# Four scalings and the convolution taps of a two-layer decoder trunk given out later

## The chip, the cores and the metric

The kernel runs on one core of one Trainium2 chip. The metric is device microseconds of one execution, and lower is better. The kernel before took 253.13 us (median of 3 runs, 252.58 to 253.38).

## The reference, cut to what matters

Two layers, each a pre-norm mixer over 256 tokens of width 1024. One input projection feeds two groups, whose outputs are joined, projected and added to the residual:

```python
h = rms_norm(x, norm_g); z = h @ w_in
# group A, width 512: gated linear recurrence
cx  = causal_depthwise_conv(rg_x, conv_w, conv_b)        # 4 taps along the tokens
r, i = sigmoid(cx @ w_r + b_r), sigmoid(cx @ w_i + b_i)  # 8 diagonal blocks of 64
a   = exp(-8 * r * softplus(-lam)); u = sqrt(1 - a*a) * (i * cx)
y_a = scan(h_t = a_t * h_(t-1) + u_t) * silu(rg_gate)
# group B, 8 query heads on 2 kv heads of 64: three attention branches
y_b = (g0 * o_compressed + g1 * o_selected + g2 * o_window) * silu(nsa_gate)
x = x + concat(y_a, y_b) @ w_out
```

At 256 tokens the selected and the window branch both see every earlier token, so each is a causal softmax over 256 keys with keys, values and a gate of its own. Products with the large weights are computed to nearly full fp32 precision as three products of a high part and a low part.

## The kernel before, in words

**Tiling.** Each layer is a list of 33 steps, and each step has one chunk of weights (128 partitions by up to 1024 columns): 13 for q, k, v and the compression inputs (`tm1`, `cmp_prod`, `tm2`), 12 "feature" chunks (`fm`, here slots 0 to 11: four for the recurrence input x0 to x3, then gate chunks), and 8 for the output projection (`out_proj`; the first four are slots 12 to 15). A feature chunk is 24 matmuls of 256 columns. Its low part `wl` is made by VectorE (L168) from the raw chunk and the high part `wh`, which ScalarE makes (L165) in slots 0 to 3 and a DMA makes from slot 4 on. The low parts are made some steps ahead; for slots 2 to 5 they stand behind the last `qs` write (L383) of the first or second half of q and k.

**What else runs in the slots.** Smaller pieces are hung into slots by `at(n, f)`: ahead of the slot's products, or, with `mid=True`, behind the loads that the slot gives out.

- `qk_transpose(t)` for the two halves t of the tokens, ahead of slots 0 and 2: TensorE transposes k and q (L369, L378) into two banks of the pool `pp` (which has two), ScalarE casts them (`kd` L373 and L374, twice each; `qs` L382, twice), VectorE makes the low parts (`kl` L375, `qs` L383), and ScalarE copies q (`qT`, L385).
- `att_scores(i, t)`: score matmuls (L579 to L581) into banks of `s` (three), the maximum on VectorE (L584, L586), and four exponentials on ScalarE (L592). Pair (0, 0) is in slot 1, pairs (0, 1) and (1, 0) in slot 3.
- `att_coef(i, t)`: a reciprocal and a product on VectorE (L597, L598), and four scalings of the probabilities on ScalarE (L605). Before, that of (0, 0) is given out in the middle of slot 1.
- `att_turn(i, t)`: four transposes of the probabilities per 128 keys on TensorE (L618) into a bank of `pp`, and their copy (L83). That of (0, 0) is ahead of slot 2.
- `cmp_act` (slot 2) and `cmp_kv` (slot 3): hidden layer of the compression, with a tanh `hth` (L468), the product `hs` (L470) on VectorE and the matmuls L475 and L476 on it.
- `rg_x(j)` behind the products of slot j: VectorE evicts x_j to `xpad` (L646; two buffers, taken in turn), ScalarE makes the tap of the newest token (`cx`, L647), VectorE adds the three others (L649). `rg_gates(j)`, ahead of slot 2 + j, multiplies `cx` with the gate weights (L657) and takes tanh and exp on ScalarE (L660 to L664).

**What sets the order.** The engines run their queues in order. The queues are filled by a planner that goes through modelled time: on each engine it takes, among the instructions that it holds ready, the one written first. So an instruction that is written later can stand ahead of one that was not yet ready in the model, and moving a statement changes the precedence of its instructions rather than fixing their places.

Of the kernel before, what the change touches and what calls it, by code (L numbers as in the profile page):

```python
# [38 lines left out]
for _n, _w in (("g", 8), ("cw", 16), ("cb", 4), ("br", 4), ("bi", 4), ("lam", 4)):  # L39
# [13 lines left out]
SL = dict(qk=(0, 2), order=("x0", "x1", "x2", "x3", "n0", "n1", "g0", "g1", "g2", "g3", "n2", "n3"),  # L53
          cmp=(2, 3, 4), att=(1, 3, 3, 4, 6, 7, 10, 11), turn=(2, 4, 5, 6, 8, 10,
          12, 13), cs=(5, 5), cpt=6, aout=(6, 7, 12, 15), gates=(2, 3, 4, 5), tab=6, sqrt=5,
          scan=8, rout=(9, 11))
# [15 lines left out]
def hybrid_trunk_kernel(ctx: ExitStack, tc: tile.TileContext, vx, wc, wt, wv, wf, wo, w1, w2, pe,  # L72
# [14 lines left out]
    def act(shape, tag, bufs=1, dt=F32):  # L87
        return ap_.tile(shape, dt, name=tag, tag=tag, bufs=bufs)
# [16 lines left out]
    xpad = [cp.tile([P, S + 4], F32, name=f"xpad{c}") for c in range(2)]  # L105
# [75 lines left out]
    def v(l, n, j=None):  # L181
        a, b = VEC_COLS[n]
        if j is not None:
            a, b = a + j, a + j + 1
        return vec[:, l, a:b]
# [70 lines left out]
    def layer(l, prev):  # L256

        L = Layer()
# [381 lines left out]
        def rg_x(j):  # L640
            if j == 0:
                L.cx = act([P, 4, S], "cx")
                L.rr = act([P, 4, S], "rr")
                L.tl = act([P, 4, S], "tl")
            cx, xp = L.cx, xpad[j % 2]
            V.tensor_tensor(xp[:, 4:], L.o[:, :S], L.rb[:, 0], op=ALU.mult)  # L646
            A.activation(cx[:, j], xp[:, 4:], AF.Identity, scale=v(l, "cw", 12 + j), bias=v(l, "cb", j))  # L647
            for k in range(3):
                V.scalar_tensor_tensor(cx[:, j], xp[:, 1 + k:1 + k + S], v(l, "cw", 4 * k + j), cx[:, j],  # L649
                                       op0=ALU.mult, op1=ALU.add)  # L650
# [115 lines left out]
        order = [(o[0], int(o[1])) for o in SL["order"]]  # L766
        base = {"x": 0, "g": 4, "n": 8}
        post = {"x": rg_x, "g": rg_gate, "n": nsa_gate}
        plan = [([], []) for _ in range(16)]

        def at(n, f, *a, mid=False):
            plan[n][1 if mid else 0].append(F(f, *a))
# [6 lines left out]
        for q in range(8):  # L779
            i, t = divmod(q, 2)  # L780
            n = SL["att"][q]
            at(n, att_scores, i, t)
            at(n, att_coef, i, t, mid=True)
        at(SL["cs"][0], cmp_scores)
        at(SL["cpt"], cmp_pt)
        for q in range(8):
            at(SL["turn"][q], att_turn, *divmod(q, 2))
        for i in range(4):
            at(SL["aout"][i], att_out, i)
            at(SL["gates"][i], rg_gates, i)  # L790
        at(SL["tab"], next_gains, mid=True)
        at(SL["sqrt"], rg_sqrt, mid=True)
# [17 lines left out]
    for l in range(DEPTH):  # L810
        prev, st_ = layer(l, prev)
        prev0 = prev0 or prev
        steps += st_
# [140 lines left out]
```

## Time and profile before

| what | value |
| --- | --- |
| median of 3 runs | 253.13 us |
| profiled execution | 252.82 us |
| its span, first to last instruction | 251.0 us |
| TensorE busy with matmuls / with weight loads | 243.0 / 222.2 us |
| VectorE, ScalarE, GpSimd busy | 195.8, 164.5, 40.1 us |
| granted TensorE clock | 1.0 over the whole span |
| memory read | 55.78 MB |

The profiled execution is 1.8 us longer than its span. Busy times are shares of the span and say how full an engine is on the mean; what an engine waited for is in the views of waits, and the order in which its queue was filled is in the timelines. In the first layer slots 0 to 5 lie at about 38 to 74 us, in the second at about 158 to 196 us.

### The profile page before, as it was taken

To read this page: it belongs to the slowest core of one execution; us is meant where nothing else is said; L and a number is where in the kernel's file an instruction comes from. 1 tells how busy PE (TensorE), PEld (TensorE's weight loads), DVE (VectorE), ACT (ScalarE), POOL (GpSimd) and SP (SyncE) were. 2 spreads that over 40 slices of the span, in tenths; PEclk is the share of its full clock that TensorE was granted. 3 is DMA by queue.
4 is the path that set the end of the run, shared out by engine and by line. 5 is a ranking of instruction groups with operands and counts; after the bars stand their busy time and mean duration, and the time that the engine had idled before them with its cause. 6 is when DMAs were issued, how large, how long until landed. Compare 5 with 4: busy or idle time off the path is not lost.

```text
span 251.0 us, 5217 instructions
## 1 busy us (share of the span) xinstructions
PE 243.0 (97%) x1958; PEld 222.2 (88%) x1958; DVE 195.8 (78%) x386; ACT 164.5 (66%) x419; POOL 40.1 (16%) x65
## 2 busy tenths in 40 slices
PE   7999998999999999999999999998999999999994
PEld 3989997977899798999999999996889879989993
DVE  4898798879999997654995569688999998765422
ACT  5966419799999967622873553849999996670000
POOL 0034460001811011000001044100100001010000
PEclk9999999999999999999999999999999999999999
DMA  6987999856699688562569878475249858833022
GB/s 211 371 289 226 318 413 407 265 168 202 195 322 403 184 266 293 174 202 72 167 207 347 312 236 263 159 230 187 93 167 347 317 177 268 271 127 84 3 84 84
DMA packets 17593, 57.17 MB, mean 228 GB/s; under 512 B 2208, under 2 KB 3360, under 8 KB 17056
## 3 DMA queue, kind: packets, MB, share of 16 engines
q1 hardware_dynamic: 12816, 39.86, 46.4%
q0 software_dynamic: 4608, 16.78, 20.9%
q8 instruction: 15, 0.25, 0.4%
q10 hardware_dynamic: 144, 0.20, 0.2%
q14 instruction: 10, 0.08, 0.1%
HBM read 55.78 MB, written 1.05 MB: 226 GB/s over the span
## 4 chain that ended last, share of the span: by engine, by line
PE 59%; DVE 19%; ACT 12%; DMA 4%; issue 2%; POOL 1%; SPq 0%; DVEq 0%; ACTq 0%
PE fm L173 11%; PE fm L175 10%; PE fm L174 10%; DVE wl L168 6%; PE s L174 4%; PE s L175 4%; PE s L173 4%; ACT pr L592 3%; PE m L628 3%; PE pp L618 3%; DMA raw<-in_wt_dram 2%; DMA raw<-in_wf_dram 2%; DVE cx L649 2%; POOL st L179 1%; DVE sm L584 1%
## 5 line engine op out<-in xcount | busy, mean ns | idle before, releaser
L168 DVE TENSOR_TENSOR wl<-raw,wh 128x1024 fp32r<-128x1024 f32 (+4 forms) x67 | 74.4, 1117 | 7.9 <-PE pp L174 3.0
L173 PE MATMUL fm<-hh,wh 128*128 128x256 f32 x192 | 56.9, 296 | 0.2
L174 PE MATMUL fm<-hl,wh 128*128 128x256 f32 x192 | 55.0, 287 | 0.0
L175 PE MATMUL fm<-hh,wl 128*128 128x256 f32 x192 | 54.5, 284 | 0.5 <-DVE wl L168 0.5
L165 ACT CAST wh<-raw 128x768 fp32r<-128x768 f32 (+4 forms) x35 | 30.8, 883 | 28.6 <-DMA raw<-in_wc_dram 7.6
L173 PEld LDWEIGHTS fm<-hh,wh 128*128 128x128 f32 x192 | 36.7, 191 | 2.1 <-issue 1.2
L175 PEld LDWEIGHTS fm<-hh,wl 128*128 128x128 f32 x192 | 36.7, 191 | 1.2 <-DVE wl L168 0.8
L174 PEld LDWEIGHTS fm<-hl,wh 128*128 128x128 f32 x192 | 36.7, 191 | 0.5 <-issue 0.4
L592 ACT ACTIVATE pr<-s,sm 128x128 f32<-128x128 f32 (+1 forms) x64 | 26.0, 417 | 9.4 <-DVE sm L586 6.0
L173 PE MATMUL fm<-yy,wh 128*128 128x256 f32 x96 | 27.4, 285 | 0.0
L175 PE MATMUL fm<-yy,wl 128*128 128x256 f32 x96 | 26.8, 279 | 0.0
L174 PE MATMUL fm<-yy,wh 128*128 128x256 f32 x96 | 26.8, 279 | 0.0
L605 ACT ACTIVATE pr<-pr,sm 128x128 f32<-128x128 f32 (+1 forms) x64 | 23.7, 455 | 1.8 <-DVE sm L598 1.8
L173 PEld LDWEIGHTS fm<-yy,wh 128*128 128x128 f32 x96 | 18.0, 188 | 1.5 <-DVE sm L597 0.8
L156 POOL DMA_DIRECT2D wh<-in_wo_dram x16 | 8.5, 530 | 66.2 <-PE fm L175 29.1
L174 PEld LDWEIGHTS fm<-yy,wh 128*128 128x128 f32 x96 | 18.1, 188 | 0.0
L175 PEld LDWEIGHTS fm<-yy,wl 128*128 128x128 f32 x96 | 18.0, 188 | 0.0
L174 PE MATMUL s<-wl,hh 128*128 128x384 f32 x48 | 16.5, 344 | 0.3 <-DVE wl L168 0.3
L723 DVE TENSOR_TENSOR head<-head,fm 128x512 f32<-128x512 f32 x11 | 7.5, 686 | 11.5 <-PE fm L175 11.5
L156 POOL DMA_DIRECT2D wh<-in_wf_dram x16 | 9.0, 565 | 46.2 <-PE fm L175 24.4
L175 PE MATMUL s<-wh,hl 128*128 128x384 f32 x48 | 16.2, 337 | 0.0
L173 PE MATMUL s<-wh,hh 128*128 128x384 f32 x48 | 15.6, 353 | 0.3 <-ACT wh L165 0.3
(205 smaller groups left out, 615.0 us busy)
## 6 DMA issues: line engine op xcount, KB each, us to landing
raw<-in_wf_dram SPq DMA_DIRECT2D x24, 512.0 KB, 4.5
wh<-in_wf_dram POOLq DMA_DIRECT2D x16, 512.0 KB, 4.8
raw<-in_wo_dram SPq DMA_DIRECT2D x16, 512.0 KB, 5.0
wh<-in_wo_dram POOLq DMA_DIRECT2D x16, 512.0 KB, 4.5
raw<-in_wt_dram SPq DMA_DIRECT2D x15, 384.0 KB, 3.9
yy<-in_w_dram SPq DMA_DIRECT2D x4, 1024.0 KB, 7.4
raw<-in_wc_dram SPq DMA_DIRECT2D x4, 512.0 KB, 5.2
raw<-in_wv_dram SPq DMA_DIRECT2D x4, 420.0 KB, 4.9
```

The source lines that it names most:

```text
L156: G.dma_start(self.wh, self.src)
L165: A.copy(hi[:, c], self.raw[:, c])
L168: V.tensor_tensor(lo[:, c], self.raw[:, c], hi[:, c].bitcast(F32), op=ALU.subtract)
L173: T.matmul(o, lh, rh, start=start, stop=False)
L174: T.matmul(o, lh, rl, start=False, stop=False)
L175: T.matmul(o, ll, rh, start=False, stop=stop)
L592: A.activation(pr[g][:, b], ov[:, b], AF.Exp, bias=sm[:, 0, 2 * g + b:2 * g + b + 1], accum_out=sm[:, 1, 2 * g + b:2 * g + b + 1])
L605: A.activation(pr[g][:, b], pr[g][:, b], AF.Copy, scale=sc_)
L618: T.transpose(pp[:, (2 * g + b) * P:(2 * g + b + 1) * P], pr[g][:, b, c * P:(c + 1) * P], ident)
L628: T.matmul(yb[g * HD:(g + 1) * HD, :S], L.vv[:, 0, b, g * HD:(g + 1) * HD], pt[:, g, b, 0:2].rearrange("p a s -> p (a s)"), start=(b == 0) ...
L649: V.scalar_tensor_tensor(cx[:, j], xp[:, 1 + k:1 + k + S], v(l, "cw", 4 * k + j), cx[:, j], op0=ALU.mult, op1=ALU.add)
L723: V.tensor_tensor(x_sb[:, m], x_sb[:, m], os_[0].rearrange("p (a s) -> p a s", a=2), op=ALU.add)
```

## The change

The four scalings of the first pair of probabilities, with their reciprocal and product, go from the middle of slot 1 to the head of slot 2, behind the second half of q and k (and behind `cmp_act`, which is hung there before). The three VectorE taps of each x_j become a piece of their own, `rg_conv(j)`: those of x0 and x1 go to the head of slot 2, those of x2 to slot 3, those of x3 to slot 4. The eviction and the newest token's tap stay behind the products of slot j. The head of slot 2 now reads, in order: `qk_transpose(1)`, `cmp_act`, `att_coef(0, 0)`, `att_turn(0, 0)`, `rg_conv(0)`, `rg_gates(0)`, `rg_conv(1)`. The heads of slots 3 and 4 end in `rg_gates(1)`, `rg_conv(2)` and in `rg_gates(2)`, `rg_conv(3)`. Both layers are changed alike, and no instruction is added or dropped.

```diff
             V.tensor_tensor(xp[:, 4:], L.o[:, :S], L.rb[:, 0], op=ALU.mult)
             A.activation(cx[:, j], xp[:, 4:], AF.Identity, scale=v(l, "cw", 12 + j), bias=v(l, "cb", j))
+
+        def rg_conv(j):
+            cx, xp = L.cx, xpad[j % 2]
             for k in range(3):
                 V.scalar_tensor_tensor(cx[:, j], xp[:, 1 + k:1 + k + S], v(l, "cw", 4 * k + j), cx[:, j],
                                        op0=ALU.mult, op1=ALU.add)
...
             at(n, att_scores, i, t)
-            at(n, att_coef, i, t, mid=True)
+            if q == 0:
+                at(SL["qk"][1], att_coef, i, t)
+            else:
+                at(n, att_coef, i, t, mid=True)
...
         for i in range(4):
             at(SL["aout"][i], att_out, i)
+            at(max(i + 1, 2), rg_conv, i)
             at(SL["gates"][i], rg_gates, i)
```

## Rows read from the trace of the kernel before

**Rows 1.** The page: busy time of each engine, then the chain by engine.
```profile
PE 243.0 (97%) x1958; PEld 222.2 (88%) x1958; DVE 195.8 (78%) x386; ACT 164.5 (66%) x419; POOL 40.1 (16%) x65
...
PE 59%; DVE 19%; ACT 12%; DMA 4%; issue 2%; POOL 1%; SPq 0%; DVEq 0%; ACTq 0%
```

**Rows 2.** Busy time by stretch; columns: stretch, length, each engine's busy us.
```profile
42.00:64.00 22.00, 21.20 (x203) 18.38 (x202) 19.03 (x43) 19.85 (x61) 3.10 (x6) 1.00 0.72 234
163.00:184.00 21.00, 19.87 (x162) 17.05 (x152) 18.75 (x43) 17.50 (x57) 2.20 (x4) 1.00 0.55 176
64.00:120.00 56.00, 56.00 (x479) 51.01 (x478) 45.55 (x80) 40.12 (x108) 9.61 (x17) 1.00 0.71 233
```

**Rows 3.** TensorE's waits, 42 to 64 us, then 163 to 184 (total, times, longest).
```profile
PE pp L618 <- DVE kl L375: 0.5, 1, 0.5
PE s L579 <- ACT pr L592: 0.3, 1, 0.3
...
PE m L475 <- DVE hs L470: 0.8, 1, 0.8
PE pp L618 <- DVE kl L375: 0.3, 1, 0.3
```

**Rows 4.** Timeline of TensorE, first layer; columns: start, duration, instruction, [idle before].
```profile
51.68 0.28 PE L174 MATMUL fm<-hl,wh 128*128 128x256 f32 x1
51.80 0.28 PE L175 MATMUL fm<-hh,wl 128*128 128x256 f32 x1
52.59 0.63 PE L618 MATMUL pp<-cst,pr 128*128 128x128 f32 x4 [0.50 <-DVE kl L375]
52.97 0.36 PE L173 MATMUL fm<-hh,wh 128*128 128x256 f32 x1
```

**Rows 5.** Timeline of VectorE, first layer.
```profile
44.54 1.22 DVE L168 TENSOR_TENSOR wl<-raw,wh 128x1024 fp32r<-128x1024 f32 x1
45.68 0.48 DVE L649 SCALAR_TENSOR_TENSOR cx<-xpad,head,cx 128x256 f32<-128x256 f32 x1
46.19 0.69 DVE L586 TENSOR_REDUCE sm<-s 128x4 f32<-128x512 f32 x1
...
50.98 1.00 DVE L649 SCALAR_TENSOR_TENSOR cx<-xpad,head,cx 128x256 f32<-128x256 f32 x2 [1.39 <-ACT cx L647]
52.01 0.43 DVE L375 TENSOR_TENSOR kl<-pp,kd 64x256 fp32r<-64x256 f32 x1
```

**Rows 6.** Timeline of ScalarE, first layer.
```profile
48.77 0.36 ACT L374 CAST kd<-pp 64x256 fp32r<-64x256 f32 x1
49.16 1.28 ACT L605 ACTIVATE pr<-pr,sm 128x128 f32<-128x128 f32 x4
50.34 0.60 ACT L647 ACTIVATE cx<-xpad,head 128x256 f32<-128x256 f32 x1
...
51.35 0.37 ACT L374 CAST kd<-pp 64x256 fp32r<-64x256 f32 x1
51.75 0.58 ACT L382 CAST qs<-pp 64x512 fp32r<-64x512 f32 x1
52.23 0.30 ACT L468 ACTIVATE hth<-m 128x160 f32<-128x160 f32 x1
```

**Rows 7.** Timeline of TensorE, second layer.
```profile
171.78 0.28 PE L175 MATMUL fm<-hh,wl 128*128 128x256 f32 x1
172.87 0.30 PE L475 MATMUL m<-w2s,hs 128*32 128x64 f32 x2 [0.82 <-DVE hs L470]
173.42 0.63 PE L618 MATMUL pp<-cst,pr 128*128 128x128 f32 x4 [0.25 <-DVE kl L375]
```

**Rows 8.** The chain that ended last, second layer: start, us, what.
```profile
167.32 1.51 ACT pr L592 x8
...
169.47 1.28 ACT pr L605 x4
```

**Rows 9.** Timeline of VectorE, second layer.
```profile
172.50 0.32 DVE L470 SCALAR_TENSOR_TENSOR hs<-hth,m 128x160 f32<-128x160 f32 x1
```

## The prediction

> **What bounds the kernel now.** I read four views, in this order. The busy table [rows 1] shows TensorE full (243.0 of 251.0 us) and the chain by engine puts 59% of the span on it; VectorE and ScalarE follow with 19% and 12%. So the end is the length of TensorE's queue plus the stalls in it, and only a stall taken out, or a new one, moves the end. The table by stretches says where there are stalls: from 64 to 120 us TensorE is busy all 56.00 us, while from 42 to 64 it idles 22.00 - 21.20 = 0.80 and from 163 to 184 it idles 21.00 - 19.87 = 1.13 [rows 2]. These two stretches are slots 1 to 4 of each layer, where the moved instructions are. There ScalarE is the next fullest (19.85 of 22.00 and 17.50 of 21.00), VectorE close to it. TensorE's waits name four: the transposes L618 of the first pair (both layers), L475 on `hs` (second layer), a score matmul on a bank that the exponentials still hold (first layer) [rows 3].
>
> What the reader is to see in the timelines is the queue order behind the waits. In the first layer ScalarE runs one half of `kd` (to 49.1), then the four scalings (49.16, 1.28 us), then x1's newest tap (50.34), and only then the other half of `kd` (to 51.7) [rows 6]. VectorE, meanwhile, stands 1.39 us at the taps of x1, which need that newest tap; `kl`, which frees the bank for L618, is queued behind two of them and starts at 52.01 [rows 5]. L618 then starts at 52.59, the matmul ahead of it at 51.80; matmuls of that kind follow each other at 0.12 us (51.68, 51.80), so the stall is 0.79 - 0.12 = 0.67 us [rows 4]. In the second layer the scalings again stand ahead (169.47 to 170.75) [rows 8], the tanh and `hs` come behind them (172.50) [rows 9], and TensorE stands 172.87 - 171.78 - 0.12 = 0.97 us for `hs` and 0.25 us more for L618 [rows 7].
>
> [...] TensorE's busy row gives 0.80 + 1.13 = 1.93 us of idle time in the two stretches. [...] The sum below stands on gaps between starts.
>
> **The change, part by part.** The profiled execution took 252.82 us (span 251.0, 1.8 around it); the median of the runs is 253.13, 0.31 above it. The sum is made against 252.82 and 0.31 is added at the end. Nothing is added or removed: 2 x 4 scalings and 2 x 12 taps change their precedence. No DMA is in a moved piece; SP and GpSimd keep their order and see only weight buffers come free at other times.
>
> *Scalings behind the second half of q and k.* ScalarE's steps are, from starts, 0.40 for a `kd` cast (51.35 to 51.75) and 0.48 for a `qs` cast (51.75 to 52.23); the newest tap is 0.60, the tanh 0.30, [rows 6]; `qT` I put at 0.48 like `qs`, an estimate. First layer: the second `kd` cast starts at 48.77, when the transposes have come, and two casts follow at once instead of after 1.28 us of scalings and a tap: three casts end at 48.77 + 1.20 = 49.97, `kl` (0.43) at 50.4 instead of 52.44. The newest tap, two `qs`, `qT` and the tanh end at 49.97 + 0.60 + 0.96 + 0.48 + 0.30 = 52.3, the scalings at 52.3 + 1.28 = 53.6. So the bank is free 2 us sooner, but the probabilities are ready 1.0 us later than L618 started before. What is late next is thus L618's own data. The cover: in the model L618 is then not ready when slot 2's products are, so it falls behind them; six of them (L173 at 52.97 and five more, 0.72 us at 0.12 [rows 4]) and the scores of pair (0, 1) are there to be run, whose `qs` is ready at 51.5 + 0.69 (VectorE's part) = 52.2, before the products end at 51.92 + 0.72 = 52.6. With the cover the 0.67 us go; without it L618 stalls TensorE 1.0 us longer. Bounds +0.67 and -1.0; I take 0.67, because the queue of before shows the planner running products ahead of transposes that were not ready.
>
> Second layer: the exponentials end at 167.32 + 1.51 = 168.83 [rows 8]. If they end 0.5 sooner (next part), four casts, tap, two `qs`, `qT` and tanh (1.60 + 0.60 + 0.96 + 0.48 + 0.30 = 3.94) end at 172.25, and `hs` (0.32) at 172.6: 0.2 us before its old end of 172.82. That is the low bound, with the tanh last. If the planner takes the tanh ahead of `qT`, or the scores of pair (0, 1) ahead of L475, the 0.97 + 0.25 = 1.22 us go whole. I take the middle, 0.7.
>
> *Taps a step later.* They cost VectorE the same 0.48 each. One goes from in front of the maximum of the first scores (45.68, maximum at 46.19 [rows 5]; the second layer repeats it), which can start a tap's 0.51 us earlier: bounds 0, if the planner fills the place with this or another tap, and 1.14, if a `wl` in front goes too. I take 0.5; it feeds ScalarE, which waits for that maximum, and is inside the figures above. The 1.39 us that VectorE stands at x1's taps go, since `kl`, `qs` and `hs` now precede them. Later taps make the gate products L657 later. I cost that at nothing: slots 3 to 5 have matmuls that do not need them, and the recurrence is used only in slots 9 and 11. If that cover is gone, the taps of x3 are late by the low part put in front of them, 1.14 us (44.54 to 45.68 [rows 5]) per layer. x2's eviction has to wait for x0's taps (same `xpad`); VectorE has from 46.9 us to the end of slot 2's products at 52.6 for three.
>
> *The score matmul that waits for its bank* (0.3 us [rows 3]) I leave as it is: it can go (0.3), because scores of (0, 1) start earlier, or grow by what TensorE comes earlier (0.67).
>
> Sum: 0.67 + 0.7 = 1.4 us; 252.82 - 1.4 = 251.4, and with 0.31, **251.7 us**.
>
> **The rivals.**
>
> *A: given back behind it, no change.* ScalarE is nearly full in the two stretches [rows 2], so TensorE, arriving 1.4 us earlier, may meet exponentials, copies and the compressed branch that come no earlier, and stand there instead. What ScalarE can gain is only its idle time there, 2.15 and 3.50 us. For it: the wait for the exponentials is already there. Against it: from 64 us on TensorE runs 56 us without idling, so it has other matmuls to take. It gives 0 to -0.5: 252.9 us.
>
> *B: slower, L618 stands at its old place in the queue.* Mechanism: the model thinks the scalings are done when L618's turn comes, and on the chip they end at 53.6, 1.0 us after L618's old start (the working is above). TensorE then idles from 51.92 to 53.6, in the first layer 1.0 us more than before; in the second the scalings end at 172.25 + 1.28 = 173.5 against 173.42, 0.1 more. It decides when fewer than 1.7 us of other matmuls (53.6 - 51.9) stand between slot 2's product at 51.80 and L618. Price 1.1: 252.82 + 1.1 + 0.31 = 254.2 us. For it: before, too, L618 stood in the queue ahead of slot 2's last six products and held them up [rows 4]. [...]
>
> *C: the order on the chip hardly changes,* because the planner takes what is ready and the casts are not, when the scalings are. Against it: the second `kd` pair comes from the same bank as the first, which ran ahead of the scalings [rows 6]. 253.1 us.
>
> **How the numbers follow.** Forecast 0.55, A 0.20, B 0.17, C 0.08. The likeliest alone reaches from 250.6 (all four waits gone, 0.67 + 1.22 + 0.3 = 2.2, and a little from the earlier maximum) to 252.5 (0.67 + 0.2, less 0.3 of a grown wait). For 8 in 10 the range takes in A, C and the near part of B: 250.5 to 253.9. About 0.3% (0.76 us) is what a measurement of this kernel can tell from no change. Faster 0.56, within 0.30, slower 0.14 (B, less its mildest part).
>
> **What would show it.** Right: on ScalarE four `kd` casts without a scaling between them, in both layers; `kl` two us sooner; no idle VectorE at x1's taps; L618 behind slot 2's last product, and no wait over 0.3 us for `hs` or L618. Wrong: L618 waiting for L605 (B); waits for exponentials or for the compressed branch that were not there (A); gate products waiting for `cx` on TensorE, which would make the tap part cost what I put at nothing. If the waits go and the time stays, the sum over stalls was the wrong measure.

## The result and the profile after

The changed kernel takes 254.45 us (median of 20 runs, 252.85 to 255.31); the kernel before, run beside it, 252.75 us (20 runs, 251.77 to 253.51). The ratio is 1.0058, 95% interval [1.0041, 1.0076]: by it the change is 1.5 us slower, where 1.4 us less was forecast. The time lies 0.55 us above the range; of the cases, rival B (254.2) is the nearest. Of the runs further down, one execution each of e7 (295.63 us, at a granted clock of 0.755), of e12 (394.82 us, at 0.561) and of the kernel before (828.99 us, beside e9 to e12) is far slower than the others of its kernel; the ratios, means and counts leave it out, the medians are over all runs.

The profiled execution took 253.98 us (span 252.2). Its page first: the busy row, the granted clock in 40 slices, and the chain by engine. They answer to [rows 1].

```profile
PE 244.1 (97%) x1958; PEld 223.7 (89%) x1958; DVE 196.2 (78%) x386; ACT 164.6 (65%) x419; POOL 40.0 (16%) x65
...
PEclk9999999999999999999999999998999999999999
...
PE 79%; ACT 9%; DVE 8%; issue 2%; DMA 1%; ACTq 0%
```

TensorE is still what sets the end, with 79% of the chain. Its busy time has grown by 1.1 us although no instruction was added, and one slice of the clock row, that from 170.2 to 176.5 us, is not full. The view by stretches, which answers to [rows 2], has both:

```profile
42.00:64.00 22.00, 20.83 (x172) 17.85 (x162) 20.08 (x47) 20.17 (x64) 4.50 (x9) 1.00 0.68 231
163.00:184.00 21.00, 19.29 (x130) 16.45 (x126) 17.22 (x41) 16.52 (x54) 2.20 (x4) 0.92 0.49 151
64.00:120.00 56.00, 55.77 (x476) 50.63 (x475) 44.46 (x75) 38.87 (x103) 8.27 (x13) 1.00 0.70 228
```

TensorE idles 1.17 us in the first layer's stretch (0.80 before) and 1.71 in the second's (1.13 before), and in the second's the mean granted clock is 0.92. TensorE's waits in the first layer (two rows), then in the second, which answer to [rows 3]:

```profile
PE pp L618 <- ACT pr L605: 0.8, 1, 0.8
PE m L497 <- DVE sm L598: 0.3, 1, 0.3
...
PE pp L618 <- DVE kl L375: 1.7, 1, 1.7
```

The wait of L475 for `hs` and that for the score bank are gone. The transposes L618 still wait, and longer: in the first layer now for the scalings, in the second for `kl`. (Lines from L649 on stand 3 lower than before: the taps are L652, the gate products L660.) TensorE's timeline in the first layer, beside [rows 4]:

```profile
49.68 0.28 PE L174 MATMUL fm<-hl,wh 128*128 128x256 f32 x1
50.73 0.33 PE L618 MATMUL pp<-cst,pr 128*128 128x128 f32 x1 [0.78 <-ACT pr L605]
50.82 0.36 PE L175 MATMUL fm<-hh,wl 128*128 128x256 f32 x1
...
51.26 0.28 PE L175 MATMUL fm<-hh,wl 128*128 128x256 f32 x1
51.64 0.33 PE L618 MATMUL pp<-cst,pr 128*128 128x128 f32 x1
```

The matmul at 49.68 is the 11th of slot 2's 24 products; before, L618 stood behind the 18th. The queue gives the four transposes out one by one between products, and TensorE stands 50.73 - 49.68 - 0.12 = 0.93 us at the first and 0.26 at the second. In the second layer, beside [rows 7], L618 stands behind the 18th product; before, it stood behind all 24 and L475:

```profile
170.50 0.28 PE L175 MATMUL fm<-hh,wl 128*128 128x256 f32 x1
172.49 0.78 PE L618 MATMUL pp<-cst,pr 128*128 128x128 f32 x4 [1.71 <-DVE kl L375]
...
174.54 0.77 PE L579 MATMUL s<-kd,qs 128*128 128x512 f32 x1
175.11 0.63 PE L580 MATMUL s<-kl,qs 128*128 128x512 f32 x1
175.54 0.44 PE L581 MATMUL s<-maskb,identb 128*128 128x256 bf16 x1
...
177.94 0.38 PE L660 MATMUL fm<-cx,rws 128*128 128x256 f32 x1
```

The stall is 172.49 - 170.50 - 0.12 = 1.87 us. What follows it is slow as well: from L579 to the gate product the scores take 177.94 - 174.54 = 3.40 us. The same instructions of the kernel before:

```profile
174.03 0.48 PE L579 MATMUL s<-kd,qs 128*128 128x512 f32 x1
174.34 0.40 PE L580 MATMUL s<-kl,qs 128*128 128x512 f32 x1
174.58 0.28 PE L581 MATMUL s<-maskb,identb 128*128 128x256 bf16 x1
...
176.03 0.60 PE L657 MATMUL fm<-cx,rws 128*128 128x256 f32 x2
```

There they take 2.00 us. The granted clock, by stretches of the changed kernel (the column behind the five engines), says why:

```profile
163.00:174.20 11.20, 9.49 (x77) 8.74 (x73) 9.38 (x18) 7.93 (x26) 0.53 (x1) 1.00 0.58 184
174.20:177.60 3.40, 3.40 (x13) 2.26 (x13) 2.18 (x5) 3.02 (x11) 1.10 (x2) 0.50 0.53 145
177.60:184.00 6.40, 6.40 (x44) 5.45 (x43) 5.66 (x20) 5.58 (x21) 0.57 (x1) 1.00 0.30 95
```

For 3.4 us, from 1.7 us after the stall's end on, TensorE's granted clock is 0.50 in place of 1.00, and the scores take 3.40 - 2.00 = 1.40 us longer. It is not in every run. Twelve of the 20 runs have a mean granted clock of 0.992 or 0.993 and a mean time of 254.68 us; the other eight have 0.998 or more and 253.53. The mean of the kernel before is 252.76. So of the mean loss of 1.46 us, 0.77 is there without the low clock, and 0.6 x 1.15 = 0.69 comes with it.

Why `kl` is late is in ScalarE's and VectorE's timelines of the second layer:

```profile
167.28 0.21 ACT L592 ACTIVATION_READ_ACCUMULATOR pr<-s,sm 128x1 f32 x1
168.26 0.40 ACT L605 ACTIVATE pr<-pr,sm 128x128 f32<-128x128 f32 x1 [0.78 <-DVE xpad L646]
168.57 0.35 ACT L373 CAST kd<-pp 64x256 fp32r<-64x256 f32 x1
168.82 0.60 ACT L647 ACTIVATE cx<-xpad,head 128x256 f32<-128x256 f32 x1
169.45 0.36 ACT L374 CAST kd<-pp 64x256 fp32r<-64x256 f32 x1
169.84 0.58 ACT L382 CAST qs<-pp 64x512 fp32r<-64x512 f32 x1
...
170.52 0.39 ACT L605 ACTIVATE pr<-pr,sm 128x128 f32<-128x128 f32 x1
170.94 0.37 ACT L373 CAST kd<-pp 64x256 fp32r<-64x256 f32 x1
171.32 0.37 ACT L374 CAST kd<-pp 64x256 fp32r<-64x256 f32 x1
```

```profile
167.81 0.42 DVE L646 TENSOR_TENSOR xpad<-fm,rb 128x256 f32<-128x256 f32 x1
169.46 0.48 DVE L652 SCALAR_TENSOR_TENSOR cx<-xpad,head,cx 128x256 f32<-128x256 f32 x1 [1.23 <-ACT cx L647]
169.86 0.41 DVE L375 TENSOR_TENSOR kl<-pp,kd 64x256 fp32r<-64x256 f32 x1
...
171.92 0.43 DVE L375 TENSOR_TENSOR kl<-pp,kd 64x256 fp32r<-64x256 f32 x1
```

The four `kd` casts (L373, L374, once for each 64 rows) don't follow each other. The pair of the second 64 rows comes 1.1 us behind the first pair (169.81 to 170.94; in the first layer it is the same, 48.19 to 49.31), after `kl` of the first 64 rows (ends at 170.27). In the program the second L373 waits for VectorE's first `kl`: e5 below, which writes the casts ahead of the differences, closes the gap (there the second L373 starts at 169.53, 0.38 us behind the L374 at 169.15). (Both read one bank of `pp`, and they share the tile `kd`; no run shows which of the two makes the cast wait.) On the chip ScalarE does not stand in the gap, since a `qs` cast, the tanh and a single scaling are queued in it. It stands at the start: the exponentials end at 167.49, but a scaling is queued ahead of the first cast and waits 0.78 us, by the trace for VectorE's eviction of x1 (L646), so the first cast starts at 168.57, 1.08 us behind the exponentials. The 1.23 us that VectorE stands at x1's tap hold `kl` up very little: it starts at 169.86, 0.05 us behind the end of the cast that it needs. From the start of the second half's L369 to the end of the last `kl` it takes 4.10 us in the first layer (before 4.46) and 5.67 in the second (before 6.05): 0.4 us less in each.

### The profile page after: what moved, and what is told of

Same layout as the page of the kernel before. It is cut to its first block, busy times and chain, and to the rows that moved or that the text cites. A ratio compares the mean times of both kernels' runs of the same rounds, so it can differ in the third digit from the quotient of the medians.

```text
span 252.2 us, 5214 instructions
## 1 busy us (share of the span) xinstructions
PE 244.1 (97%) x1958; PEld 223.7 (89%) x1958; DVE 196.2 (78%) x386; ACT 164.6 (65%) x419; POOL 40.0 (16%) x65
## 4 chain that ended last, share of the span: by engine, by line
PE 79%; ACT 9%; DVE 8%; issue 2%; DMA 1%; ACTq 0%
PE fm L173 13%; PE fm L174 12%; PE fm L175 12%; PE s L173 5%; PE s L174 5%; PE s L175 5%; PE pp L618 4%; PE m L628 3%; DVE wl L168 2%; PE s L579 2%; PE fm L660 2%; PE s L580 2%; PE pp L175 2%; PE pp L173 2%; PE pp L174 2%
## 5 line engine op out<-in xcount | busy, mean ns | idle before, releaser
L605 ACT ACTIVATE pr<-pr,sm 128x128 f32<-128x128 f32 (+1 forms) x64 | 24.3, 448 | 4.0 <-DVE sm L598 3.3
L618 PE MATMUL pp<-cst,pr 128*128 128x128 f32 x96 | 15.4, 276 | 2.6 <-DVE kl L375 1.7
```

The source lines that it names most:

```text
L605: A.activation(pr[g][:, b], pr[g][:, b], AF.Copy, scale=sc_)
L618: T.transpose(pp[:, (2 * g + b) * P:(2 * g + b + 1) * P], pr[g][:, b, c * P:(c + 1) * P], ident)
```

## The experiments

All were timed beside the kernel before, on three chips (252.40 us beside e1 to e4, 252.50 beside e9 to e12, 252.57 beside the others). In the table, the first-layer stretch goes from the start of the second half's L369 to the first product of the second layer, and the second-layer stretch from the same L369 to the last attention output (from there to the last matmul it is 27.24 us in every kernel). The stall is the longest one in slots 2 to 4 of the second layer, between starts and less the usual step. "Low" counts runs with a mean granted clock under 0.995; where a profiled execution has 0.997 to 0.999 (e4, e5, e6, e9), its clock is 1.00 from 42 to 64 us and from 160 to 190. Stretches and stalls are of one execution, times of all. The two stretches do not add up to the span, because what lies ahead of them varies: the L369 with which the first one begins starts at 47.98 us in the kernel before, at 46.41 in the changed kernel and at 47.34 in the same kernel once more (e13). Whether a part of that belongs to the change is not shown.

| kernel | median us, ratio | layer 1 | layer 2 | stall | low |
| --- | --- | --- | --- | --- | --- |
| before | | 79.38 | 52.69 | 0.97 | 0 of 84 |
| changed | 254.45, 1.0058 [1.0041, 1.0076] | 80.40 | 54.40 | 1.87 | 12 of 20 |
| changed again (e13) | 254.90, 1.0083 [1.0061, 1.0105] | 80.57 | 54.32 | 1.86 | 4 of 6 |
| scalings only (e2) | 252.87, 1.0018 [1.0000, 1.0036] | 79.92 | 52.79 | 1.35 | 0 of 12 |
| taps only (e3) | 252.80, 1.0011 [0.9994, 1.0028] | 79.45 | 52.70 | 1.58 | 0 of 12 |
| L618 in slot 3 (e1) | 252.13, 0.9981 [0.9964, 0.9999] | 79.33 | 52.57 | 0.57 | 0 of 12 |
| so in layer 1 only (e12) | 252.81, 1.0006 [0.9984, 1.0027] | 79.15 | 52.57 | 1.60 | 0 of 10 |
| so in layer 2 only (e11) | 254.04, 1.0059 [1.0044, 1.0074] | 80.12 | 52.85 | 0.58 | 0 of 5 |
| before, L618 in slot 3 (e4) | 253.60, 1.0045 [1.0025, 1.0065] | 80.43 | 52.74 | 0.95 | 0 of 12 |
| stall filled (e9) | 256.62, 1.0166 [1.0130, 1.0201] | 80.60 | 55.42 | 0.46 | 1 of 6 |
| its control (e10) | 253.78, 1.0066 [1.0043, 1.0089] | 81.57 | 52.83 | 1.88 | 4 of 10 |
| casts freed (e5) | 253.46, 1.0033 [1.0017, 1.0048] | 80.11 | 53.10 | 1.36 | 0 of 12 |
| before, casts freed (e6) | 253.30, 1.0038 [1.0016, 1.0059] | 80.46 | 52.84 | 1.29 | 0 of 12 |
| L618 in slot 3, casts freed (e7) | 251.77, 0.9956 [0.9935, 0.9978] | 79.27 | 52.12 | 0.94 | 0 of 11 |

**Is it L618's place in the queue?** e1: the changed kernel, with the transposes of (0, 0) a slot later in both layers.

```diff
-          cmp=(2, 3, 4), att=(1, 3, 3, 4, 6, 7, 10, 11), turn=(2, 4, 5, 6, 8, 10,
+          cmp=(2, 3, 4), att=(1, 3, 3, 4, 6, 7, 10, 11), turn=(3, 4, 5, 6, 8, 10,
```

> The changed kernel with the transposes of the first pair (L618) hung ahead of slot 3 instead of slot 2, so that in TensorE's queue they stand behind slot 2's 24 products and the scores of slot 3, in both layers. Theory P (place): the loss is L618 standing too early in TensorE's queue (1.87 us in the second layer, some 1.2 in the first) and the fall of the granted clock behind the second stall. Then both stalls and the fall go: 251.2 to 252.3 us, granted clock 1.0 in every run, slot 3's first product in the second layer some 2.5 us earlier than in the changed kernel. Rival S (ScalarE): the interleaved scalings and casts make ScalarE's chain late and TensorE waits for it wherever L618 stands: 253.5 to 254.5, with waits for kl, hs or exponentials of 1 us or more in slot 3. Rival T (taps): late taps hold the gate products: 253.5 to 254.5, with waits for cx.

252.13 us: by the ratios to the kernel before, 0.9981 and 1.0058, it is 0.8% (1.9 us) under the changed kernel, and a little under the kernel before. TensorE's timeline of e1, first layer:

```profile
52.15 0.28 PE L175 MATMUL fm<-hh,wl 128*128 128x256 f32 x1
52.35 0.30 PE L475 MATMUL m<-w2s,hs 128*32 128x64 f32 x2
...
52.83 0.48 PE L579 MATMUL s<-kd,qs 128*128 128x512 f32 x1
...
54.83 0.60 PE L618 MATMUL pp<-cst,pr 128*128 128x128 f32 x4
```

L618 comes behind the products and the scores, and nothing stands between. The order of ScalarE's and VectorE's casts, scalings and taps in these slots is that of the changed kernel; what differs is where L618 is queued, and its copy, and in the second layer a wait of ScalarE that is 0.27 us shorter (as in e12 below). So, with the casts and scalings in this order, the place is the cause of the stalls: L618 ahead of matmuls that could run, as rival B had it. (The products alone are not cover enough: in e3's second layer and in e6's first, L618 stands behind all 24 of them but ahead of the scores, and TensorE stands 1.58 and 1.00 us.) What is left is 0.57 us at L497 in the second layer and 0.44 at the gate products, for `cx`, in the first.

e4: the same edit on the kernel before.

> The kernel before with L618 of the first pair hung ahead of slot 3. In the first layer it then stands behind all 24 products, in the second behind L475 and a group of scores. Theory P: the old L618 stalls (0.67 and 0.25 us) go and the wait for hs in the second layer (0.97) stays: 251.8 to 252.5. Rivals S and T: no change from before, 252.5 to 253.0.

A miss: 253.60, slower than before. TensorE now stands at the first score, for VectorE's `qs`, which there has taps in front of it:

```profile
53.41 0.49 PE L618 MATMUL pp<-cst,pr 128*128 128x128 f32 x3
54.36 0.50 PE L579 MATMUL s<-kd,qs 128*128 128x512 f32 x1 [0.46 <-DVE qs L383]
```

In the second layer the 0.95 for `hs` stays. So the change and the later transposes pay only together: each alone loses (ratios 1.0058 and 1.0045), both gain a little (0.9981, with an interval that ends just under 1).

**Which part loses?** e2 leaves the taps as they were, e3 the scalings.

```diff
-            at(max(i + 1, 2), rg_conv, i)
```

(e2, with the taps back in `rg_x`)

> Only the scalings are moved, the taps stand as before. L618 then stands behind 14 of slot 2's 24 products in the first layer and 19 in the second (the changed kernel: 11 and 18; before: 18 and all 24). Theory P: most of the loss stays, 253.3 to 254.5, a stall of 1 to 2 us at L618 in the second layer, and a fall of the clock behind it in part of the runs. Rival T (taps): no loss, 252.3 to 253.0. Rival S: like P in time, but with the wait at exponentials, not at L618.

```diff
-            if q == 0:
-                at(SL["qk"][1], att_coef, i, t)
-            else:
-                at(n, att_coef, i, t, mid=True)
+            at(n, att_coef, i, t, mid=True)
```

(e3)

> Only the taps are moved, the scalings stand as before. L618 then stands behind 15 of 24 products in the first layer and behind all 24 in the second. Theory P: about the kernel before, 252.2 to 253.2, since the second layer's stall is at most the old one, and no fall of the clock. Rival T: the loss is here, 253.7 to 254.6. Rival S: as before, 252.5 to 253.0, as the scalings are not touched.

Both lose little, 0.47 and 0.40 us, and neither is set apart from no change with any margin. For e2 that is a miss: I had put most of the loss on the scalings. e3's time came as expected, its stall not. With each part alone the second layer's longest stall is longer (1.35 and 1.58 us, both at L618 for `kl`; before 0.97, at L475 for `hs`), and in neither is a run at the low clock. Their sum, 0.87, is near the 0.77 that the changed kernel loses in its runs at 0.998 or more, but each is uncertain by some 0.45 us. The other 0.69 appears only with both.

**Which layer?** e12 and e11 move the transposes in one layer.

```diff
-            at(SL["turn"][q], att_turn, *divmod(q, 2))
+            at(3 if q == 0 and not l else SL["turn"][q], att_turn, *divmod(q, 2))
```

(e12; e11 has `and l`)

> The changed kernel with L618 of the first pair ahead of slot 3 in the first layer alone. Theory P: the second layer's stall and the fall of the clock stay, 253.2 to 254.4, at most 1.2 us under the changed kernel. Rival (the first layer carries it): 252.2 to 252.8.

> The changed kernel with L618 of the first pair ahead of slot 3 in the second layer alone. Theory P (the place of L618 is the loss, and it is the second layer's stall with the clock that counts): 252.2 to 253.0, clock 1.0. Rival: the first layer's stall of 0.94 and 0.27 us carries as much: 253.3 or more.

Both missed, since I had put most of the loss on the second layer. With the first layer mended (e12) the time is that of the kernel before, and the first-layer stretch is 1.25 us shorter than the changed kernel's; the second layer's stall stays, at 1.60 us, and costs nothing that its stretch shows (52.57, before 52.69), as no run has the low clock. With the second layer mended (e11) the loss stays. So the first layer carries a loss in every run, and the low clock, where a profile shows it, lies behind the second layer's stall. That stall is 0.27 us shorter in e12 although the second layer is written as in the changed kernel: in e12 (and in e1) the scaling ahead of the first cast doesn't wait for the eviction of x1,

```profile
167.92 0.40 ACT L605 ACTIVATE pr<-pr,sm 128x128 f32<-128x128 f32 x1 [0.50 <-DVE sm L598]
```

and the last `kl` ends 5.40 us behind the L369, not 5.67. So e12 changed the second layer's stall as well, and can't say which of its two changes keeps the clock up. e11's 254.04 is 1.5 us above before, where its stretches add up to 0.9; the rest I can't place, and five runs are few.

**Is it the low clock behind the stall?** e9 fills the second layer's stall with sixteen products of 256 columns of zeros, which change no result; e10 is the same without them.

```diff
+                if k == 5 and L.fill:
+                    L.fill = False
+                    for _ in range(16):
+                        T.matmul(L.o[:, S:], wz[:, :P], wz, start=False, stop=False)
+                    att_turn(0, 0)
...
```

(Not shown is the part that arms this in the second layer alone and takes the old place out.)

> The changed kernel, in the second layer L618 tied behind 18 of slot 2's 24 products (where it stands in the changed kernel anyway), and 16 matmuls of 256 columns by zeros put in front of it, into an unused half of the products' bank. They fill the 1.87 us that TensorE stood there (16 by about 0.11 = 1.8 us) and add nothing else. Theory G (the granted clock falls because TensorE stood idle): the stall is filled, the clock stays at 1.0 in every run, and the time is that of the changed kernel's runs without a fall, 252.9 to 253.7. Rival H (the clock falls for another reason, such as what the chip does in that stretch): it falls in most runs as before, 254.0 to 255.3.

> The control of the filled kernel: the same tie of L618 behind 18 products in the second layer, without the matmuls by zeros. Theories G and H both: a stall of 1.6 to 2.0 us at L618, a fall of the clock in half or more of the runs, 253.8 to 255 in the median.

e10 is much like the changed kernel, with 253.78 us and four low runs of ten both just under what I had expected. Its first-layer stretch is 1.2 us longer than the changed kernel's, mostly since the gate products wait 1.07 us for `cx` there, so it is a control for the second layer alone. Its profiled execution has the stall, 1.88 us, but the stretch that had a clock of 0.50 there has 1.00 here (four others of its ten runs have a mean of 0.993):

```profile
174.20:177.60 3.40, 3.40 (x25) 2.42 (x23) 3.27 (x6) 3.38 (x9) 0.53 (x1) 1.00 0.18 24
```

And its second-layer stretch is 52.83, only 0.14 above before. So the wait at L618 by itself takes the place of the two waits that it removed; it is the clock, with the 1.40 us above, that makes it dear. e9 fills the gap and has no fall of the clock behind it in its profile (1.00 from 160 to 190 us), but the time is a miss, 256.62. The fill changed the order behind it: VectorE makes three `wl` in one go ahead of the next maxima.

```profile
175.48 3.49 DVE L168 TENSOR_TENSOR wl<-raw,wh 128x1024 fp32r<-128x1024 f32 x3
```

So e9 says something of the clock and nothing of the time.

**Is it the casts' interlock?** e5 issues both halves' casts ahead of VectorE's differences, for `kd` and for `qs` alike; e13 is the changed kernel once more on the same chip.

```diff
-            for g in range(2):
-                src = pk[g * HD:(g + 1) * HD, :2 * P].rearrange("p (b s) -> p b s", s=P)
+            srcs = [pk[g * HD:(g + 1) * HD, :2 * P].rearrange("p (b s) -> p b s", s=P) for g in range(2)]
+            for g, src in enumerate(srcs):
...
+            for g, src in enumerate(srcs):
...
```

> The changed kernel, with one thing undone that my forecast had overlooked: in the transposes of q and k both casts of the first and second 64 rows are issued before VectorE's two differences, so that ScalarE's second kd cast no longer waits for VectorE's first kl, nor the second qs cast for the first qs difference. Theory P (the long stall in the second layer comes of that interlock together with an early place of L618 in TensorE's queue; the early place stays): the last kl ends some 1 us sooner (about 170.9 where the changed kernel has 172.35), but the transposes now stand behind 12 of the 24 products there, 0.7 us sooner than before, and the last two scalings end near 172.2. So the stall comes apart into a wait for kl and one for L605, each under 1.3 us, together 1.3 to 2.1. Time 253.0 to 254.3, and the clock at 0.993 in few runs or none. Rival R (the interlock alone made the loss): no wait at L618 over 0.5 us, time 252.2 to 252.9. Rival G (it is the total of the idle time that brings the clock down): 0.993 in about half of the runs, 254.3 to 255.

> The changed kernel once more, unaltered, to stand beside the three others on one chip: 253.9 to 255.0, and a granted clock of 0.992 to 0.993 in 4 to 8 of its runs, with those runs 0.8 to 1.6 us above its others. If the fall of the clock were a matter of one chip and not of this kernel, it would be in none or in all of the runs.

Both came as expected in time. TensorE's and VectorE's rows of e5, second layer (lines 1 to 2 lower):

```profile
169.84 0.28 PE L175 MATMUL fm<-hh,wl 128*128 128x256 f32 x1
171.31 0.41 PE L620 MATMUL pp<-cst,pr 128*128 128x128 f32 x2 [1.19 <-DVE kl L376]
...
172.14 0.33 PE L620 MATMUL pp<-cst,pr 128*128 128x128 f32 x1 [0.19 <-ACT pr L607]
```

```profile
170.31 0.85 DVE L376 TENSOR_TENSOR kl<-pp,kd 64x256 fp32r<-64x256 f32 x2
```

The two `kl` now follow each other and end at 171.16, 4.43 us behind the L369 (166.73) and so 1.2 us sooner than in the changed kernel (0.35 of that because the first cast itself starts sooner, 1.54 us behind the L369 and not 1.89), but the transposes are queued sooner too (behind 12 products), so 1.36 and 0.35 us of wait remain. In the first layer the freed casts bring `kl` nothing: it ends 4.18 us behind the L369 (changed kernel 4.10), as VectorE has two taps of x1 in front of it, and TensorE stands 1.32 us at L618 there, for the scalings. No run has the low clock, and the time is 1.4 us under e13's. e13 shows the low clock again, in four of six runs, now 0.5 us behind the stall:

```profile
173.59 0.86 PE L618 MATMUL pp<-cst,pr 128*128 128x128 f32 x4 [1.70 <-DVE kl L375]
174.12 0.55 PE L173 MATMUL fm<-hh,wh 128*128 128x256 f32 x1
174.47 0.42 PE L174 MATMUL fm<-hl,wh 128*128 128x256 f32 x1
174.68 0.41 PE L175 MATMUL fm<-hh,wl 128*128 128x256 f32 x1
```

The products step at 0.21 us there, at a granted clock of 0.51 from 174.1 to 177.5 us; ahead of the stall they step at 0.12.

e6 is the kernel before with freed casts, e7 that of e1.

> The kernel before with the same edit of the casts alone. Theory P: the small attention product L475 now comes behind the first score products, so the 0.82 wait for hs goes, and kl is done 0.6 to 1 us sooner; 0.6 to 1.4 us is won, 251.2 to 252.0. Rival: the kernel before had these waits beside others, and they are handed on to the scalings L605 or to the maxima: 252.2 to 252.8.

> The changed kernel with the transposes L618 a slot later in both layers (252.13 by itself, where it stood under the kernel before by 0.5) and the casts freed of VectorE's differences as well. Theory P: with all 24 products ahead of the transposes the casts have their time anyway, so the freed casts bring at most 0.3 us more: 251.5 to 252.2, clock at 0.997 or above in all runs. Rival: the interlock costs its 0.5 to 1 us here too, since the first score products wait for the last kl: 250.9 to 251.5.

e6 missed: 253.30, slower. The wait for `hs` went as expected, but L618, now behind all 24 products in the first layer and behind 19 in the second, makes TensorE stand 1.00 and 1.29 us, and the first layer's wait for the score bank grew from 0.54 to 0.79. e7 came as expected, 251.77: the fastest, by 0.44% under the kernel before. Its longest waits are no longer at L618 in either layer; in the second they are:

```profile
PE s L581 <- DVE qs L385: 0.8, 1, 0.8
PE m L477 <- DVE hs L472: 0.2, 1, 0.2
```

## Why the prediction was wrong, point by point

**What bounds the kernel: right.** TensorE's queue and its stalls set the end, and the stalls lie in the two stretches. The fastest version won its time there.

**The failed step: "With the cover the 0.67 us go".** I took it that L618, once late, would fall behind slot 2's products. It went the other way: behind 11 products where it had been behind 18, and in the second layer behind 18 where it had been behind 24. I had read from [rows 4] that products run ahead of a transpose that isn't ready; the row shows just as well, as rival B said, that the queue holds a transpose ahead of products that are. The first layer lost 1.0 us in its stretch. That is also the uncovered end of my own bounds, but in part by chance, for the rows make it up of other terms: +0.52 at L618 (0.93 and 0.26 in place of 0.67), +0.42 at L497, where there was no wait, +0.3 at the gate products ahead of slot 2, and -0.54 at the score bank, whose wait went; the last 0.3 I can't place. e1 and e12 put L618 where I had thought it would go, and the loss went. Why the planner's model held L618 to be ready so soon no trace shows, and I leave it open.

**"Two casts follow at once" and "the bank is free 2 us sooner": failed too, in both layers.** The second half's casts come behind VectorE's difference of the first half, so the pairs stay 1.1 us apart, and `kl` came 0.4 us sooner, not 2. The rows of ScalarE that I read [rows 6] hold the casts of both halves in the old order too, and I had not asked what the second one waits for. I had also put no scaling ahead of the casts, and in the second layer one is there, with 0.78 us of waiting. e5 shows what the tie between the halves is worth in the second layer: freed, `kl` comes 1.2 us sooner, some 0.9 of it by the freed casts, and the longest stall is 0.5 shorter, though L618 stands earlier too. In the first layer freeing them brought nothing, so there the size of this step stays open.

**The second layer's 0.7: the `hs` wait went, as priced, and another took its place.** B's price for L618 there was 0.1; the wait was 1.87, and for `kl`, not L605. By itself it about cancels the 0.97 and 0.25 that went: e10's stretch is 0.14 above before's. The stalls themselves add up to 0.65 more, most of which comes back further on. So the second layer has next to no gain or loss at a granted clock of 1.00, in place of the 0.7 won.

**What was not in the sum at all: TensorE's clock.** [rows 2] had 1.00 in every stretch and I took it for given. In the changed kernel's two profiles 3.4 us behind the longer stall ran at a granted clock of 0.50, in e13 0.51 (1.40 us by the scores' rows of the first), and 20 of the 36 runs of the changed kernel, e13 and e10, which stall 1.86 to 1.88 us there, have the low mean clock. None of the 98 runs of the nine kernels that stall 1.60 us or less has it, nor one of the 84 of the kernel before; one of e9's six runs, at 0.991, is against the pattern. That it is the stall's length that brings it is argued from this count and from e5; no kernel changed the stall alone (in e9 the order changed with it, in e12 the first layer).

**Taps at nothing: about right in time, wrong as a cover.** They cost little alone (e3, 0.40 us, interval down to -0.15), but VectorE still stands at x1's taps in front of `kl`, where I had said that this goes: 0.21 us in the first layer (before 1.39), but 1.23 in the second (before 0.37). I had overrated it as well: in [rows 5] and [rows 6] the cast that `kl` needs ends at 51.72 and `kl` starts at 52.01, so VectorE held it up by 0.29 us at most, and ScalarE did the rest. Nor do the 1.39 us show that VectorE runs its queue in order, since the cast was not done until they were over. Other waits do show a queue's order. In the kernel before VectorE stands 2.16 us in front of L345 (31.67), while the `wl` behind it (32.60), whose high part ScalarE had made by 27.23, stands too. In the second layer of the changed kernel the second half's first `kd` cast stands behind the scaling that waits 0.78 us, though its transposes (L369) end at 167.06, and six products stand behind L618 for 1.71 us, which in e1, with L618 elsewhere, run at steps of 0.12. For GpSimd and SyncE it is not shown. The gate products did wait for `cx`, 0.3 us in the changed kernel's first layer and 1.07 in e10's.

**The rivals.** B came nearest, and I gave it 0.17, its second layer too cheap and without the clock; it had L618 at its old place, and it stood earlier than that in both layers. C is out, as the order changed. Of A there is one small sign, the 0.42 us at L497, which belongs to the compressed branch; no wait for exponentials was added.

## What to carry to other kernels

Moving a statement so that a result comes sooner moves its reader as well: before pricing a gain, find where in its queue the waiting instruction will stand, and price both ends. When a producer's steps read two halves of one bank on two engines, look for the wait between the halves before adding their durations up (here the pairs of casts came 1.1 us apart). And a stall of 1.87 us on TensorE had a second price here beside its length, where the granted clock dropped to 0.50 behind it (1.40 us); read the clock in every run, not in one profile.

## What was not expected of the hardware

In two profiles the granted clock fell for 3.4 us after TensorE had stood for 1.87 us (the changed kernel) and 1.86 us (e13): to 0.50 from 174.2 to 177.6 us of the span in the first, from 1.7 us behind the stall's end on, and to 0.51 from 174.1 to 177.5 us in the second, from 0.5 us behind it. The mean clock is low in 12 of 20 and 4 of 6 runs of the changed kernel and in 4 of 10 of e10, and in none of 98 runs of kernels whose longest stall there is 1.6 us or less. One of e9's six runs, with the stall filled, has 0.991. A stall of 1.88 us in e10's profile had no fall behind it (1.00 from 160 to 190 us), and each of the two kernels has runs with the low mean and without, so the kernel alone does not decide it.
